# A hybrid decoder layer on one core: weight parts kept in DRAM after their first split, modulation tiles moved, eight differences on GpSimd

## The chip, the core and the metric

One core of a Trainium2 chip runs the whole layer. The metric is device time in microseconds, the median of several runs. Five engines work side by side, each through its own queue in order: TensorE (PE), VectorE (DVE), ScalarE (ACT), GpSimd (POOL) and SyncE (SP), which issues every DMA of this kernel, all into one queue.

## What is computed

One decoder layer over 2048 tokens of width 1024, in float32:

```python
mod = silu(c) @ w_ada + b_ada          # six vectors: shift, scale, gate, twice
h = rms_norm(x, ln1_g) * (1 + sc1) + sh1
p = h @ w_in                           # 3600 columns: qa fa ia ga | qb kb vb gb rb
o = concat(hgrn2(qa, fa, ia, ga), gla(qb, kb, vb, gb, rb))   # two gated linear recurrences, 4 heads each
x = x + gt1 * (o @ w_out)
h = rms_norm(x, ln2_g) * (1 + sc2) + sh2
u = causal_dwconv(h @ w_up)            # 5632 columns, 3 taps
a, v = split(u)
x = x + gt2 * ((silu(a) * v) @ w_down)
return rms_norm(x, lnf_g)
```

## The kernel before, in words

**Split operands.** A float32 matrix product is made of three passes. Each operand is cut into a rounded high part and the remainder (`hi`, `lo`), and `split_passes` multiplies hi by hi, hi by lo and lo by hi. `split_into` (L124 to L131) makes the parts: a ScalarE cast (L128) and a VectorE subtraction (L131). Nearly every weight tile is 128 x 1024 (a `ga` tile 128 x 1056), so one weight means one cast and one subtraction, and then 24 matmuls of 512 columns.

**Blocks.** The tokens are worked in four blocks of 512 (`plan_A(s)`, s = 0 to 3), two per half (`sgi`). A block's mixer is a list of steps, made with `add(names, mm, kind)`: `names` are the weights that the step needs, `mm` issues its matmuls. Mixer order: `f0` to `f3`, `ga`, `kb0 qb0 kb1 qb1`, `ia`, `q0`, `vb`, `q1` to `q3`, `gb`, then `o0` to `o7`. `ga`, `ia`, `vb` and `gb` are token sections: four weights, held through four steps, one per group of 128 tokens. Block 0 differs: its `f` and `kb` weights come as eight start tiles `s0` to `s7` (128 x 768, array `ws`), one per 128 rows of the contraction, whose low parts POOL subtracts. So a block has 36 weights of its own, used again in each of the four blocks.

After the mixers of two blocks comes the up-product of that half (`plan_ffn`): five plain feature pairs (`ua`, `uv`, ten weights) for the first block, seventeen pairs for both blocks by Strassen's scheme (kind `"own"`, weights prepared by `weights_first` and its helpers, L1211 and L1215; matmuls L1222), and the same five plain pairs for the second block. Then the down-product, also by Strassen's scheme (L1553), and the final norm (`finish`, L1668). The ten plain weights are thus used four times.

**What sets the order.** `at(i, fn)` hangs other work on step i: the scan stages of the recurrences, norms, gates. ACT and SP issue in program order; DVE, PE and POOL are ordered by the compiler's scheduler, except in the start and the `"own"` steps, which are written out by hand. Weights run through two cursors over the list `seq` of all names: `w_dma(upto)` (L1776) loads raw tiles into the pool `bigp` (12 buffers), `w_split(upto)` (L1791) splits them into the pool `wsp` (4 pairs hi/lo). The main loop (L1872 on) splits what a step needs, for an `"early"` step two more weights before its matmuls, for a `"late"` one after them, and loads up to three raw tiles beyond that. `mid(k)` (L1836) is the same for start step k: it loads the modulation weights of step k+3 (`ada1_load`), raw tile k+4, and splits s(k+1).

**Modulation.** `ada_tile(j, k)` (L227) adds 128 rows of `w_ada` to two accumulators on VectorE (L229), 4 x 8 tiles of two 128 x 512 instructions. `plan_ada` (L1737) hangs the tiles of j = 2 on every second step of block 0 from `ga1`, those of j = 4, 3, 5 on the 24 steps from the second one of block 1; each tile is loaded one step ahead into the pool `slots` (62 buffers of 128 x 512), which nearly all other tiles share.

**Strassen operands.** `build` (L1153) makes sums and differences of the two blocks' normed activations in the four x1 tiles of each block (in `bigp`, loaded by `resid_load` at step `q3`). T3 and T4 are four VectorE differences each (L1171, L1175), then split.

Of the kernel before, what the change touches and what calls it, by code (L numbers as in the profile page):

```python
# [13 lines left out]
ALU = mybir.AluOpType  # L14
# [15 lines left out]
GW = T + RK  # L30
LEAD = 96
WBUF = 1152

EPS = 1e-6
TINY = 2.0 ** -63
# [27 lines left out]
def kernel(  # L63
# [41 lines left out]
    def slot(dt=F32):  # L105
        return slots.tile([P, T], dt, tag="s", name="s")

    def big():
        return bigp.tile([P, 2 * GW], F32, tag="big", name="big")

    def bank():
        return psp.tile([P, T], F32, tag="ps", name="ps")
# [71 lines left out]
    def load_rest():  # L184
        pool.tensor_copy(ones_r, ones)
        sp.dma_start(g2_sb, g2)
        sp.dma_start(lb_sb, lbp)
        gk_raw = slot()[0 : 3 * RK, 0:256]
        sp.dma_start(gk_raw, wgk)
        act.copy(wgk_sb, gk_raw)  # L190
        lo = slice(2 * RK, 3 * RK)
        vec.tensor_tensor(wgk_sb[lo], gk_raw[lo], wgk_sb[lo].bitcast(F32), op=ALU.subtract)
        sp.dma_start(bgk_sb, bgk)
        sp.dma_start(gna_sb, gna)
        sp.dma_start(gnb_sb, gnb)
# [10 lines left out]
        vec.tensor_scalar(omlb, lb_sb, -1.0, 1.0, op0=ALU.mult, op1=ALU.add)  # L206

    ada_acc = {}

# [121 lines left out]
    side = defaultdict(list)  # L331
    inner = defaultdict(list)

    def add(names, mm, kind="early"):

        steps.append((names, mm, kind))
        return len(steps) - 1

    def at(i, fn):
        side[i].append(fn)  # L340
# [432 lines left out]
    def plan_A(s, hurry):  # L773
# [59 lines left out]
        def section(name, banks, src=h):  # L833

            w4 = []
            wide = name == "ga"
            stride = GW if wide else T
            cuts = [(0, T // 2), (T // 2, GW)] if wide else [(0, T)]

            def token(tt):  # L840
                def mm(w):
                    w4.extend(w)
                    pts = [bank() for _ in cuts]
                    m = 0
                    for kp in range(4):
                        if kp == 2:
                            run_half()
                        for k2 in range(2):
                            for hv, wv in split_passes(src[2 * kp + k2], w4[kp]):
                                for pt, (c0, c1) in zip(pts, cuts):  # L850
                                    pe.matmul(  # L851
                                        pt[:, 0 : c1 - c0],
                                        lhsT=hv[:, tt * P : (tt + 1) * P],
                                        rhs=wv[:, k2 * stride + c0 : k2 * stride + c1],
                                        start=(m == 0),
                                        stop=(m == 23),
                                    )
                                m += 1
                    banks.append(pts if wide else pts[0])

                return mm

            for tt in range(NT):
                names = [f"{name}{i}" for i in range(4)] if tt == 0 else []
                tick[f"{name}{tt}"] = add(names, token(tt), "hold" if tt < NT - 1 else "late")

        section("ga", bga)
        for j in range(2):
# [188 lines left out]
        at(tg + 1, u1.stage_f2)  # L1057
        at(tg + 2, lambda: u1.stage_g(oT))

        at(tick["q3"], lambda: resid_load(s))  # L1060

        def out_evac(j):
            xt = x1_of(s, j)
# [23 lines left out]
            return hT[self.s][k]  # L1087

    cap = [None]
    between = []  # L1090

    def names_before(i):
# [2 lines left out]
    def plan_ffn(sg):  # L1095
# [245 lines left out]
        def strassen(f, prev, nxt, nxt2, prev2):  # L1341
# [70 lines left out]
            def t6():  # L1412
# [8 lines left out]
                if nxt2 is not None:  # L1421
                    load_u(nxt2)
                if nxt is None:
                    w_split(cur[1] + 2)

            def s_cap():
                if nxt is None:
                    cap[0] = names_before(info["i1"] + FILL)
                    for k in range(4):
                        back.append(slot())  # L1430
                        sp.dma_start(back[k], h12_d[sg][k])
                    w_dma(cur[1] + 3)

            def t0_():
                s_cap()
# [178 lines left out]
        def unit(u):  # L1614
# [3 lines left out]
            def mm(w):  # L1618
# [29 lines left out]
                        del op[ci, p, k]  # L1648
                if sg == 0 and u == len(units) - 4:
                    cap[0] = None  # L1650
                    w_dma(cur[1] + 2)
                if sg == 0 and u == len(units) - 2:
                    w_split(cur[1] + 2)

            return mm

# [75 lines left out]
        for n in range(4):  # L1732
            at(i1 + n, lambda n=n: norm2_T(s, (2 * n, 2 * n + 1)))

    ada_seq = [(j, k) for j in (2, 4, 3, 5) for k in range(KD)]

    def plan_ada(i0, i1):  # L1737
        def one(j, k):
            if k == 0:
                ada_start(j)  # L1740
            ada_tile(j, k)

        for n, (j, k) in enumerate(ada_seq):
            i = i0 + 2 * n if j == 2 else i1 + n - KD
            at(i - 1, lambda j=j, k=k: ada_load(j, k))
            at(i, lambda j=j, k=k: one(j, k))
            if k == KD - 1:
                at(i + 2, lambda j=j: ada_norm2(j, range(0, 4)))
                at(i + 3, lambda j=j: (ada_norm2(j, range(4, 8)), ada_acc.pop(j)))

    for sgi in range(2):
        s0, s1 = 2 * sgi, 2 * sgi + 1
        tick0, end0 = plan_A(s0, False)
        if sgi == 0:
            plan_ada(tick0["ga0"] + 1, end0 + 1)
        plan_norm1(s1, tick0["gb0"], tick0["gb3"] + 1)
        tick1, end1 = plan_A(s1, True)
        plan_norm2(s0, tick1["gb3"] + 1)
        info = plan_ffn(sgi)
        if sgi == 0:  # L1760
            s2, i5 = s1 + 1, info["last"]
# [12 lines left out]
    RAW_AHEAD, SPLIT_AHEAD = 4, 2  # L1774

    def w_dma(upto):  # L1776
        while cur[0] < min(upto, len(seq) if cap[0] is None else cap[0]):
            i = cur[0]
            t_ = big()
            if seq[i][0] == "s":  # L1780
                t_ = t_[:, 0 : 6 * P]
                sp.dma_start(t_, ws[int(seq[i][1:])])
            elif seq[i][:2] == "ga":
                sp.dma_start(t_, wg[int(seq[i][2:])])
            else:
                t_ = t_[:, 0:D]
# [1 line left out]
            raws[i] = t_  # L1788
            cur[0] += 1

    def w_split(upto):  # L1791
        while cur[1] < min(upto, len(seq) if cap[0] is None else cap[0]):
            i = cur[1]
            w_dma(i + 1)
            hi, lo = (wsp.tile([P, WBUF], F32R, tag=f"w{c}", name=f"w{c}") for c in ("hi", "lo"))
            hi, lo = hi[:, 0 : 2 * GW], lo[:, 0 : 2 * GW]
            raw = raws.pop(i)
            n = raw.shape[-1]
            split_into(hi[:, 0:n], lo[:, 0:n], raw, lo_engine=pool if seq[i][0] == "s" else None)
            wsplit[i] = (hi, lo)  # L1800
            cur[1] += 1


# [11 lines left out]
    with tc.manual_schedule(engines={ENG.Activation, ENG.DVE, ENG.PE, ENG.Pool, ENG.SP}):  # L1815
# [48 lines left out]
        keep_warm(1)  # L1864
        for k in range(KD):
            steps[k][1]([wsplit.pop(k)])
            ptr += 1
        del xn1[0]

    for i, (names, mm, kind) in enumerate(steps):  # L1870
# [7 lines left out]
        if kind == "unit":  # L1878
# [1 line left out]
                fn()  # L1880
            mm(None)
            continue
        w_split(ptr + len(names))
        w = [wsplit.pop(ptr + n) for n in range(len(names))]
        ptr += len(names)
        if kind == "early":
# [6 lines left out]
        run_half()  # L1893
        if kind == "late":
            w_split(ptr + 2)
    for fn in side.pop(len(steps), ()):
# [88 lines left out]
```

## Time and profile before

| | us |
|---|---|
| median of 3 runs (lowest to highest) | 2381.95 (2381.03 to 2382.35) |
| profiled execution, its own time | 2378.33 |
| its span, first to last instruction | 2376.6 |
| mean granted TensorE clock | 0.988 |

PE is matmuls, PEld weight loads; times in rows are microseconds from the span's start, and "mean ns" is that of one instruction. A wait is named by the waiting engine and line, the tile, and what ended it. Matmuls are pipelined and their ends modelled, so the busy time of PE says little; the distance between matmuls says more. In this execution the start and block 0's mixer lie in 0 to 283 us, block 1's mixer in 283 to 537, the first half's plain up-products in 537 to 604, its Strassen part in 604 to 918, the second plain pass in 918 to 976, the down-product to 1200; blocks 2 and 3 lie in 1200 to 1452 and 1452 to 1697, the second half's plain up-products in 1697 to 1765.

### The profile page before, as it was taken

How to read it: one execution, taken by the hardware profiler on the slowest of the kernel's cores; microseconds unless marked ns; L12 is line 12 of the kernel's file. 1: busy time of each engine (PE TensorE's matmuls, PEld its weight loads, DVE VectorE, ACT ScalarE, POOL GpSimd, SP SyncE). 2: the span in 40 equal slices, each digit the busy share in tenths (PEclk: the TensorE clock that was granted, in tenths of full speed). 3: DMA queues.
4: the chain of work that ended last, by engine and by line, in shares of the span. 5: the costliest groups of instructions: out<-in, count | busy, mean ns of one | idle time of the engine just before them, and what ended most of it. 6: DMA issues, size and time to landing. Idle time of an engine off the chain costs nothing.

```text
span 2376.6 us, 33021 instructions
## 1 busy us (share of the span) xinstructions
PE 2299.3 (97%) x12310; PEld 1904.7 (80%) x12310; DVE 1838.8 (77%) x2787; ACT 1179.6 (50%) x2095; POOL 341.0 (14%) x312
## 2 busy tenths in 40 slices
PE   8999999999999999999989999999989999999996
PEld 6878787887788888888777888888878888888885
DVE  6687778868787888987876776577697878897778
ACT  5644544365555455544545454545555455445353
POOL 3342234110000000000224314320100000000001
PEclk9999999999999999999999999999999999999998
DMA  8233353323222247996534124221322222489751
GB/s 307 106 126 116 119 219 105 119 92 134 76 93 102 93 142 250 344 336 217 181 122 159 36 111 170 72 90 54 131 86 94 102 101 101 175 306 375 247 192 71
DMA packets 148705, 360.84 MB, mean 152 GB/s; under 512 B 17544, under 2 KB 20024, under 8 KB 148544
## 3 DMA queue, kind: packets, MB, share of 16 engines
q1 hardware_dynamic: 148544, 358.73, 42.3%
q8 instruction: 96, 1.57, 0.3%
q14 instruction: 65, 0.53, 0.1%
HBM read 293.65 MB, written 65.01 MB: 151 GB/s over the span
## 4 chain that ended last, share of the span: by engine, by line
PE 74%; DVE 16%; ACT 4%; issue 4%; DMA 2%; POOL 0%; SPq 0%; DVEq 0%; ACTq 0%; POOLq 0%
PE ps L1222 26%; PE ps L1553 14%; PE ps L363 13%; PE ps L851 11%; PE ps L886 3%; DVE wlo L131 3%; DVE s L131 2%; DMA s<-in_w_ada 1%; PE ps L709 1%; PE ps L708 1%; ACT whi L128 1%; DVE s L1668 1%; PE ps L682 1%; PE ps L816 1%; DVE s L1579 1%
## 5 line engine op out<-in xcount | busy, mean ns | idle before, releaser
L1222 PE MATMUL ps<-s,whi 128*128 128x512 f32 x1904 | 586.2, 389 | 3.7 <-DVE big L1322 2.4
L363 PE MATMUL ps<-s,whi 128*128 128x512 f32 x1568 | 492.4, 396 | 11.8 <-ACT whi L128 11.8
L131 DVE TENSOR_TENSOR wlo<-big,whi 128x1024 fp32r<-128x1024 f32 (+3 forms) x290 | 343.6, 1194 | 134.4 <-ACT whi L128 130.6
L1222 PEld LDWEIGHTS ps<-s,whi 128*128 128x128 f32 x1904 | 357.0, 188 | 79.2 <-DVE big L1322 3.2
L1553 PE MATMUL ps<-s,whi 128*128 128x512 f32 (+1 forms) x1272 | 385.4, 385 | 4.7 <-DVE s L131 3.0
L1222 PE MATMUL ps<-s,wlo 128*128 128x512 f32 x952 | 369.9, 389 | 2.4 <-DVE wlo L1215 2.4
L363 PEld LDWEIGHTS ps<-s,whi 128*128 128x128 f32 x1568 | 294.9, 190 | 77.6 <-ACT whi L128 14.4
L128 ACT CAST whi<-big 128x1024 fp32r<-128x1024 f32 (+3 forms) x298 | 275.2, 939 | 145.6 <-PE ps L1553 25.5
L851 PE MATMUL ps<-whi,s 128*128 128x512 f32 (+2 forms) x1280 | 339.9, 354 | 5.5 <-ACT whi L128 5.5
L455 POOL TENSOR_TENSOR s<-s 128x512 f32<-128x512 f32 (+1 forms) x69 | 102.8, 1489 | 1545.5 <-DMA big<-in_wd 588.4
L363 PE MATMUL ps<-s,wlo 128*128 128x512 f32 x784 | 307.8, 394 | 3.1 <-DVE wlo L131 3.1
L1553 PEld LDWEIGHTS ps<-s,whi 128*128 128x128 f32 x1272 | 238.3, 190 | 54.0 <-DVE s L131 4.7
L1553 PE MATMUL ps<-s,wlo 128*128 128x512 f32 (+1 forms) x636 | 244.9, 386 | 5.0 <-DVE wlo L131 4.9
L851 PEld LDWEIGHTS ps<-whi,s 128*128 128x128 f32 x1280 | 218.2, 189 | 37.8 <-ACT whi L128 7.2
L851 PE MATMUL ps<-wlo,s 128*128 128x512 f32 (+2 forms) x640 | 205.0, 351 | 6.5 <-DVE wlo L131 6.5
L1222 PEld LDWEIGHTS ps<-s,wlo 128*128 128x128 f32 x952 | 178.7, 188 | 40.4 <-DVE wlo L1215 3.2
L363 PEld LDWEIGHTS ps<-s,wlo 128*128 128x128 f32 x784 | 148.6, 189 | 36.3 <-DVE wlo L131 4.9
L1215 DVE TENSOR_TENSOR wlo<-big,whi 128x1024 fp32r<-128x1024 f32 (+1 forms) x136 | 145.1, 1083 | 5.9 <-ACT whi L1211 5.6
L1211 ACT CAST whi<-big 128x1024 fp32r<-128x1024 f32 (+1 forms) x136 | 127.5, 939 | 37.4 <-DVE big L1199 33.8
L1553 PEld LDWEIGHTS ps<-s,wlo 128*128 128x128 f32 x636 | 120.6, 190 | 30.5 <-DVE wlo L131 7.4
L1267 DVE SCALAR_TENSOR_TENSOR big<-big,cw_sb 128x1024 f32<-128x1024 f32 x68 | 87.3, 1284 | 68.2 <-ACT big L1259 68.2
L851 PEld LDWEIGHTS ps<-wlo,s 128*128 128x128 f32 x640 | 113.6, 189 | 21.9 <-DVE wlo L131 8.5
(220 smaller groups left out, 3277.5 us busy)
## 6 DMA issues: line engine op xcount, KB each, us to landing
big<-in_wt SPq DMA_DIRECT2D x230, 512.0 KB
s<-td SPq DMA_DIRECT2D x110, 256.0 KB
big<-in_wd SPq DMA_DIRECT2D x72, 384.0 KB
s<-actd SPq DMA_DIRECT2D x98, 256.0 KB
s<-in_w_ada SPq DMA_DIRECT2D x96, 256.0 KB
big<-in_wd SPq DMA_DIRECT2D x72, 320.0 KB
actd<-big SPq DMA_DIRECT2D x34, 512.0 KB
td<-s SPq DMA_DIRECT2D x54, 256.0 KB
```

The source lines that it names most:

```text
L128: act.copy(hi, src)
L131: (lo_engine or vec).tensor_tensor(lo, src, hi.bitcast(F32), op=ALU.subtract)
L363: pe.matmul(pt, lhsT=wv[:, k * P : (k + 1) * P], rhs=hv, start=(n == 0), stop=(n == 3 * KD - 1))
L455: engine.tensor_tensor(acc, acc, sq, op=ALU.add)
L682: pe.matmul(ub[lo:hi, p * P : (p + 1) * P], lhsT=self.kt[:, p * P + lo : p * P + hi], rhs=v[p][:, col : col + P], start=True, stop=True,)
L851: pe.matmul(pt[:, 0 : c1 - c0], lhsT=hv[:, tt * P : (tt + 1) * P], rhs=wv[:, k2 * stride + c0 : k2 * stride + c1], start=(m == 0), stop=(m ...
L886: pe.matmul(pout[j][0], lhsT=wv[:, k * P : (k + 1) * P], rhs=hv, start=(k == 0 and m == 0), stop=(k == KD - 1 and m == 2),)
L1211: act.copy(dst[f][0][:, 0:n], src[f][:, 0:n])
L1215: vec.tensor_tensor(lo[:, 0:n], src[f][:, 0:n], hi[:, 0:n].bitcast(F32), op=ALU.subtract)
L1222: pe.matmul(pt, lhsT=wv[:, c0 : c0 + P], rhs=hv, start=(start and n == 0), stop=(n == 11), skip_group_check=not start)
L1267: vec.scalar_tensor_tensor(t_, src[:, 1 : 1 + D], w1, t_, op0=ALU.mult, op1=ALU.add)
L1553: pe.matmul(pt[:, cols], lhsT=wv[:, ki * P : (ki + 1) * P], rhs=hv[:, cols], start=(start and n == 0), stop=(n == 3 * np_ - 1), skip_group ...
```

## The change

Three edits and what they need. **Weights:** at its first use a weight is split as before; SP then stores both parts in DRAM (`w_flush`), and every later use loads the parts instead of the raw tile, with no cast and no subtraction. The start tiles' parts are stored as the `f0` to `f3`, `kb0`, `kb1` tiles that later blocks use, in pieces of 128 columns. Parts go into the four `wsp` pairs and, where `big_pairs` allows (2 or 4 in blocks 1 to 3 and around the plain up-products), into pairs of big buffers; `live` and `last_use` keep account of which step uses a weight last. **Modulation:** the tiles of j = 4, 3, 5 leave out the steps `qb1` to `q0` of block 1 and go on later instead; accumulators are opened two steps ahead. **Differences:** T3 and T4 of the first half are computed by POOL. Also: `resid_load` moves from `q3` to `gb0`, one buffer less in `slots`, big buffers of 1088 columns.

```diff
-    slots = ctx.enter_context(tc.tile_pool(name="slots", bufs=62))
+    slots = ctx.enter_context(tc.tile_pool(name="slots", bufs=61))
...
-        add(["o0", "o1"], parts((0, 1), (0, 1)))
-        add(["o2", "o3"], parts((2, 3), (0, 1)), "hold")
+        add(["o0", "o1"], parts((0, 1), (0, 1)), last=(3, 4))
+        add(["o2", "o3"], parts((2, 3), (0, 1)), "hold", last=(4, 5))
...
-        at(tick["q3"], lambda: resid_load(s))
+        at(tick["gb0"], lambda: resid_load(s))
+        at(tick["gb0"], lambda: big_pairs.__setitem__(0, 2))
+        if s:
+            at(base, lambda: big_pairs.__setitem__(0, 2 if s % 2 else 4))
+        at(end, lambda: big_pairs.__setitem__(0, 0))
...
+            spare = vec if sg else pool
...
-                    vec.tensor_tensor(src[k], x1_of(s1, k + 4), src[k], op=ALU.subtract)
+                    spare.tensor_tensor(src[k], x1_of(s1, k + 4), src[k], op=ALU.subtract)
...
-                    vec.tensor_tensor(src[k], src[k], s0k[k], op=ALU.subtract)
+                    spare.tensor_tensor(src[k], src[k], s0k[k], op=ALU.subtract)
...
-            plan_ada(tick0["ga0"] + 1, end0 + 1)
+            plan_ada((2,), range(tick0["ga0"] + 1, end0, 2))
...
+            busy = range(tick1["qb1"], tick1["q0"] + 1)
+            plan_ada((4, 3, 5), [i for i in range(end0 + 1, end1) if i not in busy])
...
+    START = [f"f{h}" for h in range(4)] + ["kb0", "kb1"]
+    ws_d = [dram.tile([P, 6, D], F32, name=f"wsd{c}") for c in range(2)]
...
+    def w_flush(n=None):
+        for dst, src in wstores[:n]:
+            sp.dma_start(dst, src.bitcast(F32))
+        del wstores[:n]
...
+    def w_load_one(i, bigs_only=False):
+        kinds = list(live.values())
+        if kinds.count("wsp") < 4 and not bigs_only:
+            live[i] = "wsp"
+            hl = [wsp.tile([P, WBUF], F32R, tag=f"w{c}", name=f"w{c}") for c in ("hi", "lo")]
+        elif kinds.count("big") < big_pairs[0]:
+            live[i] = "big"
+            hl = [big(F32R) for _ in range(2)]
+        else:
+            return False
...
+            sp.dma_start(t_.bitcast(F32), src)
...
+    def w_load(bigs_only=False):
+        while cur[1] < limit() and is_loaded(cur[1]) and w_load_one(cur[1], bigs_only):
+            cur[1] += 1
+            cur[0] = max(cur[0], cur[1])
...
+            if seq[i][0] == "s":
+                k = int(seq[i][1:])
+                for c, t_ in enumerate((hi, lo)):
+                    wstores.append((ws_d[c][:, :, k * P : (k + 1) * P], t_.rearrange("p (j c) -> p j c", c=P)))
+            elif seq[i] in again:
+                for c, t_ in enumerate((hi, lo)):
+                    wstores.append((part_of(seq[i], c), t_))
...
             w_dma(k + 4)
+            w_flush()
             w_split(k + 2)
...
         w_dma(min(ptr + 4, cur[1] + 3))
+        w_flush(None if steps[i + 1 : i + 2] and steps[i + 1][2] == "own" else stored)
         due.extend(halfway.pop(i, ()))
         mm(w)
         run_half()
+        w_used(i)
+        w_load()
```

## Rows read from the trace of the kernel before

**Rows 1.** The page, part 1: busy us, share of the span, instructions per engine.

```profile
PE 2299.3 (97%) x12310; PEld 1904.7 (80%) x12310; DVE 1838.8 (77%) x2787; ACT 1179.6 (50%) x2095; POOL 341.0 (14%) x312
```

**Rows 2.** Chain of waits in order of time, 601 to 914: start us, us, what.

```profile
601.45 311.75 PE ps L1222 x1374
```

**Rows 3.** Waits of PE, 283 to 604: us in total, times, longest us.

```profile
PE ps L363 <- ACT whi L128: 4.2, 1, 4.2
PE ps L851 <- ACT whi L128: 2.5, 1, 2.5
PE ps L851 <- DVE wlo L131: 2.4, 1, 2.4
...
PE ps L767 <- DVE s L756: 1.0, 1, 1.0
...
PE ps L363 <- DVE wlo L131: 0.3, 1, 0.3
```

**Rows 4.** Waits of PE, 1200 to 1765, the same columns.

```profile
PE ps L363 <- ACT whi L128: 4.9, 2, 4.2
PE ps L851 <- DVE wlo L131: 4.1, 3, 1.4
PE ps L851 <- ACT whi L128: 3.0, 4, 1.3
PE ps L767 <- DVE s L756: 2.3, 2, 1.4
PE ps L363 <- DVE wlo L131: 1.8, 1, 1.8
PE ps L1222 <- DVE wlo L1215: 1.2, 1, 1.2
PE ps L1222 <- ACT whi L1211: 1.2, 1, 1.2
```

**Rows 5.** Groups of instructions: count | busy us, mean ns | idle before us, what ended it.

```profile
L131 DVE TENSOR_TENSOR wlo<-big,whi 128x1024 fp32r<-128x1024 f32 x162 | 214.8, 1342 | 65.0 <-ACT whi L128 61.6
...
L128 ACT CAST whi<-big 128x1024 fp32r<-128x1024 f32 x162 | 164.4, 1042 | 31.3 <-PE ps L363 18.0 <-PE ps L851 10.2 <-DMA big<-in_wt 3.0
...
L1171 DVE TENSOR_TENSOR big<-big 128x512 f32<-128x512 f32 x8 | 5.5, 682 | 0.0
```

**Rows 6.** Windows: us; PE, PEld, DVE, ACT, POOL busy; PEclk, DMA share, GB/s.

```profile
283.00:537.00 254.00, 246.94 (x1654) 208.98 (x1653) 191.96 (x328) 118.08 (x241) 70.80 (x64) 0.99 0.40 142
915.00:976.00 61.00, 59.82 (x264) 49.20 (x264) 57.41 (x84) 31.99 (x51) 10.70 (x7) 1.00 0.84 290
361.40:368.20 6.80, 5.39 (x14) 4.27 (x15) 6.80 (x9) 0.29 (x1) 3.38 (x4) 0.50 0.12 39
583.20:590.00 6.80, 5.25 (x12) 4.01 (x13) 6.68 (x13) 5.87 (x9) 0.00 (x0) 0.50 0.18 50
1743.80:1747.20 3.40, 3.11 (x7) 2.35 (x8) 3.28 (x8) 3.40 (x7) 0.00 (x0) 0.50 0.00 0
```

**Rows 7.** Transfers, 8 to 40 us: queue, packets, MB, share of 16 engines.

```profile
q1 hardware_dynamic: 6491, 12.71, 104.0%
```

**Rows 8.** Timeline of ACT at 583 us: start us, us, instruction, idle before.

```profile
583.13 0.63 ACT L1127 ACTIVATE s<-s 128x512 f32<-128x512 f32 x1 [6.78 <-DVE s L1123]
```

**Rows 9.** Timeline at 259 us, DVE and POOL.

```profile
259.69 3.45 DVE L131 TENSOR_TENSOR wlo<-big,whi 128x1024 fp32r<-128x1024 f32 x2
...
259.91 4.37 POOL L455 TENSOR_TENSOR s<-s 128x512 f32<-128x512 f32 x2 [39.00 <-ACT s L454]
```

**Rows 10.** Timeline of DVE at 553 us.

```profile
553.04 2.36 DVE L131 TENSOR_TENSOR wlo<-big,whi 128x1024 fp32r<-128x1024 f32 x2
```

**Rows 11.** Timeline of ACT at 48 us.

```profile
48.34 0.91 ACT L269 ACTIVATE s<-s,c_sb 128x256 f32<-128x256 f32 x2
```

**Rows 12.** Waits of SP's queue, 283 to 537: us in total, times, longest us.

```profile
SPq L224 <- PE ps L658: 11.5, 1, 11.5
```

More of the change, by code (lines that the diff above doesn't have):

```diff
@@ L32 @@
 WBUF = 1152
+BBUF = 1088
 EPS = 1e-6
@@ L106, in slot, with big @@
         return slots.tile([P, T], dt, tag="s", name="s")
-    def big():
-        return bigp.tile([P, 2 * GW], F32, tag="big", name="big")
+    def big(dt=F32):
+        return bigp.tile([P, BBUF], dt, tag="big", name="big")
     def bank():
@@ L332, with add @@
     inner = defaultdict(list)
-    def add(names, mm, kind="early"):
+    last_use = {}
+    def add(names, mm, kind="early", last=0):
         steps.append((names, mm, kind))
+        n0 = sum(len(st[0]) for st in steps[:-1])
+        for n in range(len(names)):
+            last_use[n0 + n] = len(steps) - 1 + (last[n] if isinstance(last, tuple) else last)
         return len(steps) - 1
@@ L864, in section @@
                 names = [f"{name}{i}" for i in range(4)] if tt == 0 else []
-                tick[f"{name}{tt}"] = add(names, token(tt), "hold" if tt < NT - 1 else "late")
+                tick[f"{name}{tt}"] = add(names, token(tt), "hold" if tt < NT - 1 else "late", NT - 1)
         section("ga", bga)
@@ L1089 @@
     cap = [None]
+    big_pairs = [0]
     between = []
@@ L1650, in mm @@
                     cap[0] = None
-                    w_dma(cur[1] + 2)
-                if sg == 0 and u == len(units) - 2:
-                    w_split(cur[1] + 2)
+                    big_pairs[0] = 4
+                    w_load(bigs_only=True)
             return mm
@@ L1733, in plan_norm2, with plan_ada @@
             at(i1 + n, lambda n=n: norm2_T(s, (2 * n, 2 * n + 1)))
[L1735 to L1749, printed above, removed]
+    def plan_ada(js, at_steps):
+        it = iter(at_steps)
+        for j in js:
+            for k in range(KD):
+                i = next(it)
+                if k == 0 and j != 2:
+                    at(i - 2, lambda j=j: ada_start(j))
+                at(i - 1, lambda j=j, k=k: ada_load(j, k))
+                at(i, lambda j=j, k=k: ada_tile(j, k))
+            at(i + 2, lambda j=j: ada_norm2(j, range(0, 4)))
+            at(i + 3, lambda j=j: (ada_norm2(j, range(4, 8)), ada_acc.pop(j)))
     for sgi in range(2):
@@ L1773, with part_of, is_loaded, limit @@
     cur = [0, 0]
-    RAW_AHEAD, SPLIT_AHEAD = 4, 2
+    START = [f"f{h}" for h in range(4)] + ["kb0", "kb1"]
+    ws_d = [dram.tile([P, 6, D], F32, name=f"wsd{c}") for c in range(2)]
+    parts_d = {}
+    first_use = {}
+    for i, n in enumerate(seq):
+        first_use.setdefault(n, i)
+    again = set()
+    for i, n in enumerate(seq):
+        if n in START or first_use[n] != i:
+            again.add(n)
+    def part_of(n, c):
+        if n in START:
+            return ws_d[c][:, START.index(n)]
+        if (n, c) not in parts_d:
+            w = 2 * GW if n[:2] == "ga" else D
+            parts_d[n, c] = dram.tile([P, w], F32, name=f"wp{n}_{c}")
+        return parts_d[n, c]
+    def is_loaded(i):
+        return seq[i][0] != "s" and (seq[i] in START or first_use[seq[i]] != i)
+    live = {}
+    now = [0]
+    wstores = []
+    def w_flush(n=None):
+        for dst, src in wstores[:n]:
+            sp.dma_start(dst, src.bitcast(F32))
+        del wstores[:n]
+    def limit():
+        return len(seq) if cap[0] is None else cap[0]
+    def w_used(step):
+        for i in [i for i in live if last_use[i] <= step]:
+            del live[i]
+    def w_load_one(i, bigs_only=False):
[8 more added lines that the diff above has]
+            return False
+        res = []
+        for c, t_ in enumerate(hl):
+            src = part_of(seq[i], c)
+            t_ = t_[:, 0 : src.shape[-1]]
+            sp.dma_start(t_.bitcast(F32), src)
+            res.append(t_)
+        wsplit[i] = tuple(res)
+        return True
+    def w_load(bigs_only=False):
+        while cur[1] < limit() and is_loaded(cur[1]) and w_load_one(cur[1], bigs_only):
+            cur[1] += 1
+            cur[0] = max(cur[0], cur[1])
     def w_dma(upto):
-        while cur[0] < min(upto, len(seq) if cap[0] is None else cap[0]):
+        while cur[0] < min(upto, limit()):
             i = cur[0]
+            if is_loaded(i):
+                break
             t_ = big()
@@ L1789, in w_dma, with w_split @@
             cur[0] += 1
-    def w_split(upto):
-        while cur[1] < min(upto, len(seq) if cap[0] is None else cap[0]):
+    def w_split(upto, need=False):
+        while cur[1] < min(upto, limit()):
             i = cur[1]
+            if is_loaded(i):
+                if not w_load_one(i):
+                    assert not need, seq[i]
+                    return
+                cur[1] += 1
+                cur[0] = max(cur[0], cur[1])
+                continue
             w_dma(i + 1)
             hi, lo = (wsp.tile([P, WBUF], F32R, tag=f"w{c}", name=f"w{c}") for c in ("hi", "lo"))
-            hi, lo = hi[:, 0 : 2 * GW], lo[:, 0 : 2 * GW]
             raw = raws.pop(i)
             n = raw.shape[-1]
-            split_into(hi[:, 0:n], lo[:, 0:n], raw, lo_engine=pool if seq[i][0] == "s" else None)
+            hi, lo = hi[:, 0:n], lo[:, 0:n]
+            split_into(hi, lo, raw, lo_engine=pool if seq[i][0] == "s" else None)
+            live[i] = "wsp"
             wsplit[i] = (hi, lo)
+            if seq[i][0] == "s":
[5 more added lines that the diff above has]
+                    wstores.append((part_of(seq[i], c), t_))
             cur[1] += 1
@@ L1882 @@
             continue
-        w_split(ptr + len(names))
+        stored = len(wstores)
+        w_split(ptr + len(names), True)
         w = [wsplit.pop(ptr + n) for n in range(len(names))]
```

9 lines of the change are left out of this document (7 added, 2 removed).

## The prediction

> **What bounds the kernel now.** The page's busy line comes first: TensorE 97%, VectorE 77%, ScalarE 50% [rows 1]. The 97% overstates how full TensorE is, because matmuls overlap; the chain of waits gives the pace. In the first half's Strassen blocks 1374 matmuls follow one another in 311.75 us, 0.227 us each [rows 2]: nothing but TensorE is left there, and a change can only save in the other stretches. So the third view is the list of who ended TensorE's idle time, by stretch. In 283 to 604 us (mixer of block 1, then the plain up-products) and in 1200 to 1765 us (mixers of blocks 2 and 3, plain up-products of the second half) most of that time ends at a cast (`whi`, line 128) or a subtraction (`wlo`, line 131) that splits a weight [rows 3, 4]. The work behind these waits is 1.34 us of VectorE and 1.04 us of ScalarE per weight [rows 5]. The last view is the windows with the granted clock: around such waits the clock stands at 0.5, the 1.2 GHz level, for 3.4 or 6.8 us [rows 6].
>
> **The change, part by part.**
>
> *Splits removed.* Blocks 1 to 3 each use 36 mixer weights that block 0 has used before, and the up-products use ten weights four times, so 3 x 36 + 3 x 10 = 138 casts and 138 subtractions go: 138 x 1.34 = 185 us of VectorE and 138 x 1.04 = 144 us of ScalarE [rows 5]. Almost all of it lies beside TensorE's work; what counts is the waits. Of weights that will be loaded as parts, 283 to 537 us has 2.5 + 2.4 + 0.3 = 5.2 us (the 4.2 us on line 363 in the same view is a first use and stays split) [rows 3], and 1200 to 1765 us has 4.9 + 4.1 + 3.0 + 1.8 = 13.8 us [rows 4]. Together **-19.0 us**.
>
> *The clock.* Four stretches at half clock follow those waits: one of 6.8 us and three of 3.4 us (from 361.4, 1204.5, 1286.4 and 1743.8 us; the first and the last are shown) [rows 6]. TensorE is busy for most of them, and each busy microsecond at 1.2 GHz does half a microsecond's work: 17 us / 2, less the idle part, **-8 us**. They go only if nothing else idles TensorE just before.
>
> *Waits on a less loaded VectorE.* In the same stretches line 767 waits 1.0 + 2.3 us for gated outputs, and line 1222 1.2 + 1.2 us for the first Strassen weights of the second half [rows 3, 4]. In front of both, the two engines have weight splits in their queues, four `o` weights or the plain weights. Bounds 0 and -5.7 us; I take half, **-3 us**, because the gate's own chain of sigmoid, product and transpose stays.
>
> *What takes the splits' place.* SyncE now issues two part loads per weight, 1.05 MB against 0.52 MB. With the transfer engines full they move 12.71 MB in 32 us, 397 GB/s [rows 7], so a pair of parts takes 2.6 us, while its 24 matmuls take 24 x 0.227 = 5.4 us [rows 2]. The mixer of block 1 moves 142 GB/s now [rows 6]; 36 x 0.52 MB more in 254 us makes 216. The densest stretch is the plain up-products at 915 to 976 us, 290 GB/s [rows 6]: 10 x 0.52 MB more gives 376, below 397. The Trainium skill ("DMA: Bandwidth & Descriptors", Specifications) puts a core's share of HBM at about 358 GB/s; by that figure this pass would end some 3 us late, an estimate, but the row gives 397 and decides. The loads are asked for up to six or eight weights ahead (four pairs, and two or four in big buffers). A section's four pairs come free one by one during its last token step, as each weight's last matmul is done, so a burst starts about 4 us before the section ends. Queued behind a part load that waits for TensorE are the next modulation tiles, the x1 stores and, in the up-products, the stores of activations; VectorE waits for the first of these. Bounds: 0, and for each of the 12 token sections of blocks 1 to 3 one pair's 2.6 us, 31 us. I take **+1 us**: the nearest rows are today's raw weights, asked for about as far ahead, and no wait of TensorE there ends at a load [rows 3, 4]; besides, the modulation tiles leave out the steps (`qb1` to `q0`) in which SyncE would sit on a slot.
>
> *Stores in the first 60 us.* The eight start weights are stored as parts in rows of 512 bytes, 0.79 MB per weight, in the same queue as the loads, which is full from 8 to 40 us (104% of its 16 engines) [rows 7]. Four of these pairs go ahead of the last modulation load (mid(0) to mid(3)): 4 x 0.79 MB / 397 GB/s = 7.9 us if short rows cost nothing extra. I count that load as landed when the full stretch ends, at 40 us; it is first read at 48.34 us [rows 11], so 8 us are covered. Lower bound 0. Upper bound: each 512-byte packet costs what the mean packet of that stretch costs (32 us x 1.04 x 16 engines / 6491 packets = 82 ns) [rows 7], 1536 packets / 16 x 82 ns = 7.9 us per weight, four of them 31 us, less 8, +23 us. I take **+2 us**, near the lower end, since packets of different size do not cost the same. The other stores, 30 weights of block 0 and ten of the first plain pass at 1.05 MB each, lie beside matmuls; a pair is reused four weights later, 4 x 5.4 us on, against 2.6 us for its store. I take **+1 us**, bounds 0 and +5 (two stores' time).
>
> *Eight differences by Pool* (T3 and T4, first half only). VectorE loses 8 x 0.68 = 5.4 us [rows 5] at a place where it decides: ScalarE sat 6.78 us until VectorE's convolution was done (583.13 us) [rows 8], and only then cast the weights for which TensorE waited 4.2 us [rows 3], with 6.8 us of half clock on top [rows 6]. But Pool and VectorE hinder each other. Two subtractions took 3.45 us beside Pool's additions [rows 9] and 2.36 us without [rows 10]: 1.1 us for one encounter. Eight would cost 8.7 us, net +3.3; with none it is -5.4. The Trainium skill ("SBUF — State Buffer", Who interferes with whom) says that a VectorE instruction with two SBUF inputs and a GpSimd one that reads SBUF exclude each other for a whole instruction; the rows agree in kind. The convolutions read PSUM, so part of the encounters fall away. I take **0**, between the ends.
>
> *Modulation tiles and other moves.* The same 24 x 2 products are spread over steps that had none; the residual loads move one step later, past q3. No wait of TensorE names either: 0, with +/-2.
>
> **Sum.** -19 - 8 - 3 + 1 + 2 + 1 + 0 = -26 us against the profiled execution's 2378.3 us (span 2376.6): 2352.3. The median of the runs lies 3.6 us above that execution, so I forecast **2356 us**. Differences within 0.2%, 4.8 us, I call no change, about what a measurement here can tell.
>
> **Rivals.**
>
> *A. The waits move.* With splits gone, TensorE meets the scan chain, which is just behind: the gate, `sprev`, the transposes. For it: line 767 waits already now [rows 3, 4]. Against: VectorE is freed of 185 us. If half of the 19 + 8 us come back, 2356 + 13.5 = 2369. Chance 0.17.
>
> *B. Pool holds VectorE.* The differences run back to back while VectorE is saturated, each one holding it for its whole length; TensorE's 4.2 us wait grows. By the rows +3.3 us, with a longer half clock of 3.4 us: 2363. By the rule that the Trainium skill states there, taken literally, VectorE loses the time of eight whole Pool instructions (4.37 / 2 = 2.19 us each beside VectorE [rows 9]), 17.5 us, less 5.4: +12, 2368. Chance 0.15.
>
> *C. The start is held by the short-row stores:* halfway to the upper bound, +10 us, 2366. For it: the queue is full [rows 7]. Chance 0.10.
>
> *D. Slower: part loads come late.* SyncE issues in order. A modulation tile waited up to 11.5 us for a slot in block 1 [rows 12]; a part load queued behind it starts late, and TensorE then waits at the head of a token section. One pair (2.6 us) plus the half clock after it (1.7 us of loss) at each of 12 sections is 52 us: 2356 + 52 = 2408. It decides from 26 / 12 = 2.2 us per section on. Against: the six steps left out, and the lead of 4 us. Chance 0.12.
>
> *E. Nothing moves:* the waits were only the last of several, within 5 us of 2382. Chance 0.06.
>
> My forecast itself has 0.40: 2345 to 2363 by its own bounds.
>
> **How the numbers follow.** Faster is the forecast with A, B and C: 0.82, less 0.01 for their upper tails, 0.81. Same is E with that tail, 0.07. Slower is D, 0.12. The range runs down to 2336 (the +4 us of costs not paid, the other 2.7 us of the freed waits, 5.4 us by the differences and with them the rest of the first half's plain wait and its clock, some 7 us) and up to 2384, just beyond E's middle; D's case lies outside.
>
> **What would show it.** Right: lines 128 and 131 at 128x1024 fall from 162 to 36 instructions; TensorE's waits on `whi` and `wlo` of lines 363 and 851 are gone outside block 0 and the first plain pass; the four half-clock stretches are missing; HBM traffic grows by 138 x 0.52 MB read and some 48 MB written, 120 MB; what now lies in 283 to 537 us is some 8 us shorter (5.2 of waits, 2.7 of clock), what lies in 1200 to 1765 us some 18 to 20. Wrong: TensorE waits whose releaser is a load of a part (D); a start weight's step later than 65 us (C); a wait longer than 4.2 us before the first Strassen block (B); line 767 or 709 waiting more than now (A).

## The result and the profile after

The changed kernel takes **2354.66 us** (median of 4 runs, 2350.73 to 2356.85) against 2381.49 us in the same measurement (4 runs): ratio 0.9889, 95% interval 0.9877 to 0.9900, so 1.0 to 1.2% less. The forecast was 2356. Its profiled execution took 2356.09 us, span 2354.0.

The page of the changed kernel, part 1 and the traffic of part 3, against [rows 1]:

```profile
PE 2291.7 (97%) x12310; PEld 1904.2 (81%) x12310; DVE 1672.2 (71%) x2641; ACT 1050.9 (45%) x1957; POOL 333.0 (14%) x320
HBM read 366.20 MB, written 113.38 MB: 204 GB/s over the span
```

The page of before has 293.65 MB read and 65.01 written, so traffic grows by 72.6 + 48.4 = 121 MB. VectorE loses 167 us of work and ScalarE 129 (the prediction had 185 and 144 for the splits); the span loses 22.6. The groups of 128 x 1024 splits, against [rows 5] (lines of the layer's code stand 1 to 14 lower in the file than before: 128 is 129, 851 is 858, 1553 is 1567):

```profile
L132 DVE TENSOR_TENSOR wlo<-big,whi 128x1024 fp32r<-128x1024 f32 x36 | 48.2, 1360 | 10.8 <-ACT whi L129 9.4 <-DMA wpua<-whi 0.7 <-ACT big L538 0.3
L129 ACT CAST whi<-big 128x1024 fp32r<-128x1024 f32 x36 | 36.5, 1042 | 11.8 <-DMA big<-in_wt 5.3 <-PE ps L370 4.6 <-PE ps L858 1.1
```

Both traces hold 12310 matmuls, so they can be cut at the same ones in order of time. The stretches below are those of the front part; lengths in us, by the prediction's own terms.

| stretch (before) | before | after | found | forecast |
|---|---|---|---|---|
| start, 2 to 66 | 63.8 | 64.4 | +0.6 | +2 |
| block 0, 66 to 283 | 217.0 | 221.9 | +4.9 | +1 |
| block 1, 283 to 537 | 254.0 | 247.9 | -6.1 | some -8 |
| plain up-products, 537 to 604 | 67.0 | 71.1 | +4.1 | 0 |
| Strassen, 604 to 918 | 313.9 | 313.9 | 0.0 | 0 |
| plain pass and down-product, 918 to 1200 | 282.4 | 283.1 | +0.7 | 0 |
| blocks 2, 3 and plain, 1200 to 1765 | 564.6 | 539.3 | -25.3 | -18 to -20 |
| the rest | 611.6 | 610.3 | -1.3 | 0 |

The spans of these two executions differ by 22.6 us, their own times by 22.2, where the prediction's sum, which starts from this execution of the kernel before, has 26. The medians differ by 26.8: the traced execution of before lies 3.2 us under its median, that of after 1.4 above, and this difference is in no stretch of the table. No stretch with a large term came out exactly: more was saved behind 1200 us, and 9 us were given back in two places that the prediction had put at 1 and 0.

Waits of PE in the changed kernel, 288 to 604 us (us in total, times, longest), against [rows 3]:

```profile
PE ps L370 <- ACT whi L129: 9.8, 1, 9.8
PE ps L715 <- DVE s L679: 2.5, 1, 2.5
PE ps L619 <- POOL s L601: 0.7, 2, 0.4
...
PE ps L774 <- DVE s L763: 0.2, 1, 0.2
```

The 5.2 us for weights that now come as parts (lines 851 and 363 before, 858 and 370 now) are gone. New is a wait for masked scores (line 679), and the wait of 4.2 us before the first Strassen block is now 9.8. The same view of 1204 to 1744 us, against [rows 4]:

```profile
PE ps L476 <- DVE s L132: 1.1, 2, 0.9
PE ps L1235 <- ACT whi L1224: 1.0, 1, 1.0
PE ps L619 <- POOL s L601: 0.7, 2, 0.4
PE ps L774 <- DVE s L763: 0.2, 1, 0.2
```

All 13.8 us of weight waits are gone here. Windows of the changed kernel, columns as in [rows 6]:

```profile
582.10:595.80 13.70, 6.20 (x14) 4.63 (x15) 13.58 (x25) 5.93 (x9) 1.26 (x1) 0.50 0.32 107
141.80:148.60 6.80, 6.58 (x24) 4.72 (x25) 5.17 (x8) 0.00 (x0) 2.01 (x2) 0.50 1.00 392
288.40:536.30 247.90, 243.96 (x1654) 206.84 (x1653) 148.04 (x295) 85.55 (x208) 59.18 (x62) 1.00 0.62 226
921.30:978.10 56.80, 56.80 (x251) 46.86 (x250) 41.57 (x72) 21.14 (x35) 10.07 (x7) 1.00 0.99 366
```

The four half-clock stretches that the prediction named are gone, but the one before the first Strassen block has doubled to 13.7 us, and block 0 has one of 6.8 us at 141.8, where the kernel before has one of 3.4 us at 129.3. Block 1 moves 226 GB/s (216 forecast). The densest pass runs at 366 GB/s with the transfer engines 99% busy and TensorE without a gap: 56.8 us, shorter than the 58.1 before. The 358 GB/s of the Trainium skill ("DMA: Bandwidth & Descriptors", Specifications), by which the prediction's estimate had it end 3 us late, are exceeded without harm.

### The profile page after: what moved, and what is told of

Same layout as the page of the kernel before. It is cut to its first block, busy times and chain, and to the rows that moved or that the text cites. A ratio compares the mean times of both kernels' runs of the same rounds, so it can differ in the third digit from the quotient of the medians.

```text
span 2354.0 us, 32995 instructions
## 1 busy us (share of the span) xinstructions
PE 2291.7 (97%) x12310; PEld 1904.2 (81%) x12310; DVE 1672.2 (71%) x2641; ACT 1050.9 (45%) x1957; POOL 333.0 (14%) x320
## 5 line engine op out<-in xcount | busy, mean ns | idle before, releaser
L1235 PE MATMUL ps<-s,whi 128*128 128x512 f32 x1904 | 586.2, 389 | 1.0 <-ACT whi L1224 1.0
L1235 PEld LDWEIGHTS ps<-s,whi 128*128 128x128 f32 x1904 | 357.2, 188 | 76.1 <-ACT whi L1224 1.4
L1235 PE MATMUL ps<-s,wlo 128*128 128x512 f32 x952 | 369.8, 389 | 0.0
L370 PE MATMUL ps<-s,whi 128*128 128x512 f32 x1040 | 325.5, 395 | 10.8 <-ACT whi L129 10.8
L1567 PEld LDWEIGHTS ps<-s,whi 128*128 128x128 f32 x1272 | 239.3, 190 | 55.9 <-DVE s L132 4.7
L858 PE MATMUL ps<-whi,s 128*128 128x512 f32 (+1 forms) x992 | 252.6, 345 | 0.0
L370 PEld LDWEIGHTS ps<-s,whi 128*128 128x128 f32 x1040 | 194.4, 189 | 53.3 <-ACT whi L129 12.0
L132 DVE TENSOR_TENSOR wlo<-big,whi 128x768 fp32r<-128x768 f32 (+3 forms) x152 | 161.8, 1070 | 73.7 <-ACT whi L129 71.8
L1235 PEld LDWEIGHTS ps<-s,wlo 128*128 128x128 f32 x952 | 178.7, 188 | 36.9
L370 PE MATMUL ps<-s,wlo 128*128 128x512 f32 x520 | 203.4, 392 | 1.5 <-DVE wlo L132 1.5
L370 PE MATMUL ps<-s,big 128*128 128x512 f32 x792 | 185.6, 391 | 0.0
L129 ACT CAST whi<-big 128x768 fp32r<-128x768 f32 (+3 forms) x160 | 134.5, 848 | 106.5 <-DVE big L1548 26.3
L370 PEld LDWEIGHTS ps<-s,big 128*128 128x128 f32 x792 | 147.8, 188 | 31.7 <-issue 1.3
L858 PE MATMUL ps<-wlo,s 128*128 128x512 f32 (+2 forms) x496 | 150.3, 341 | 3.1 <-DVE wlo L132 3.1
L1567 PEld LDWEIGHTS ps<-s,wlo 128*128 128x128 f32 x636 | 120.9, 190 | 29.9 <-DVE wlo L132 6.7
```

What stands on the lines that cost most here:

```text
L129: act.copy(hi, src)
L132: (lo_engine or vec).tensor_tensor(lo, src, hi.bitcast(F32), op=ALU.subtract)
L370: pe.matmul(pt, lhsT=wv[:, k * P : (k + 1) * P], rhs=hv, start=(n == 0), stop=(n == 3 * KD - 1))
L858: pe.matmul(pt[:, 0 : c1 - c0], lhsT=hv[:, tt * P : (tt + 1) * P], rhs=wv[:, k2 * stride + c0 : k2 * stride + c1], start=(m == 0), stop=(m ...
L1235: pe.matmul(pt, lhsT=wv[:, c0 : c0 + P], rhs=hv, start=(start and n == 0), stop=(n == 11), skip_group_check=not start)
L1567: pe.matmul(pt[:, cols], lhsT=wv[:, ki * P : (ki + 1) * P], rhs=hv[:, cols], start=(start and n == 0), stop=(n == 3 * np_ - 1), skip_group ...
```

## Experiments

Each kernel was timed in alternation with the kernel before (2380 to 2382 us in each group of runs); intervals of 95% are those of the ratio to it. A stretch's length is from one profiled execution; lengths of the start differ by up to 4 us among these kernels (62.9 to 66.7) with nothing in the edits to explain it, so a difference of that size needs a wait beside it. Expectations name some runs by label: e1_vec is the differences back on VectorE, e4_mod_back the changed kernel with the modulation tiles on their old steps, e8_start4 the accumulators opened earlier.

### The differences back on VectorE

```diff
-            spare = vec if sg else pool
+            spare = vec
```

> The changed kernel with T3 and T4 of the first half back on VectorE. Theory (GpSimd's differences hold VectorE's two-SBUF-input work before the first Strassen block): the wait on line 370 at 589.6 us falls from 9.99 to 4 or 5 us, its half clock from 13.7 to 6.8 us, and the time falls by 4 to 7 us, to 2348 to 2351. Rival (the longer wait comes from the weights' side, stores that hold the pairs): the wait stays at about 10 us or grows by VectorE's 5.4 us, time 2354 to 2360.

2348.81 us, ratio 0.9863 (0.9848 to 0.9879), as the theory has it, and 5.8 us below the changed kernel's median, measured in another group of runs; 537 to 604 us takes 66.9 us instead of 71.1, with this wait and a half-clock stretch of 6.8 us:

```profile
PE ps L370 <- ACT whi L129: 5.3, 1, 5.3
```

The mechanism is in VectorE's timeline. In the changed kernel it does 12 two-operand instructions (sums and low parts) while GpSimd does the eight differences:

```profile
570.30 5.18 DVE L1179 TENSOR_TENSOR big<-big 128x512 f32<-128x512 f32 x3
575.41 1.78 DVE L132 TENSOR_TENSOR s<-big,s 128x512 fp32r<-128x512 f32 x1
577.11 1.77 DVE L1179 TENSOR_TENSOR big<-big 128x512 f32<-128x512 f32 x1
578.80 7.52 DVE L132 TENSOR_TENSOR s<-big,s 128x512 fp32r<-128x512 f32 x7
586.24 0.74 DVE L1131 SCALAR_TENSOR_TENSOR s<-ps,cw_sb,s 128x511 f32<-128x511 f32 x1
```

That is 586.24 - 570.30 = 15.9 us. With the differences on VectorE the same point of its queue comes after 19 instructions (the same 12 and seven of the differences), 571.30 to 582.74 us, 11.4 us, 0.60 each:

```profile
571.30 1.89 DVE L1179 TENSOR_TENSOR big<-big 128x512 f32<-128x512 f32 x3
573.11 0.68 DVE L132 TENSOR_TENSOR s<-big,s 128x512 fp32r<-128x512 f32 x1
573.71 0.68 DVE L1179 TENSOR_TENSOR big<-big 128x512 f32<-128x512 f32 x1
...
582.74 0.74 DVE L1131 SCALAR_TENSOR_TENSOR s<-ps,cw_sb,s 128x511 f32<-128x511 f32 x1
```

So 12 instructions that need 12 x 0.60 = 7.2 us took 15.9: VectorE lost 8.7 us to eight GpSimd instructions, 1.1 us each, which is the prediction's price for one encounter, paid eight times. At this point VectorE is 15.9 - 11.4 = 4.5 us later, and the stretch is 4.2 us longer; the rest of the 5.8 us between the medians the traces do not place.

### The differences alone

The kernel before, with T3 and T4 of the first half on GpSimd and nothing else.

> The kernel before with the eight differences on GpSimd and nothing else. Theory (GpSimd holds VectorE): slower by 4 to 7 us, 2385 to 2389, all of it between 580 and 605 us. The prediction's term: 0, 2381.5, with bounds 2376 and 2385. By the rule of whole-instruction exclusion taken literally: +12, 2393.

2384.31 us, ratio 1.0010 (1.0001 to 1.0020): slower by 0.2 to 4.8 us. The stretch 537 to 604 us grows by 3.3 us, and TensorE's wait there from 4.2 to 9.3:

```profile
PE ps L363 <- ACT whi L128: 9.3, 1, 9.3
```

The median lies just under the theory's range, and 3.3 us is the prediction's upper bound: eight encounters at 1.1 us less the 5.4 us that VectorE no longer works. The traces also say where the 1.1 us come from. In the changed kernel's stretch, shown above, VectorE's instructions start 1.70 us apart (575.41, 577.11, 578.80), though each needs only 0.60: about 1.1 us of a GpSimd instruction goes between two of VectorE's. With VectorE idle, GpSimd adds two tiles of the same size in 1.29 us:

```profile
274.54 1.29 POOL L462 TENSOR_TENSOR s<-s 128x512 f32<-128x512 f32 x1 [2.66 <-ACT s L461]
```

So the two take turns, each for nearly a whole instruction. The rule of the Trainium skill ("SBUF — State Buffer", Who interferes with whom) fits this in kind, and nearly in size. The 17.5 us that the prediction drew from it used 2.19 us per GpSimd instruction, a length taken beside VectorE that by this reading contains GpSimd's own waiting; eight times 1.29 are 10.3 us, and the trace has 8.7.

### The modulation tiles, without the parts and with them

First the kernel before with the modulation tiles on their new steps; then the changed kernel with the tiles on their old steps. Both runs move the opening of the accumulators together with the tiles.

```diff
-            plan_ada(tick0["ga0"] + 1, end0 + 1)
+            plan_ada((2,), range(tick0["ga0"] + 1, end0, 2))
...
+            plan_ada((4, 3, 5), [i for i in range(end0 + 1, end1) if i not in busy])
```

> The kernel before with the modulation tiles' new steps alone (accumulators opened two steps ahead). The prediction's term: 0 within 2 us, 2379.5 to 2383.5. Rival (the new waits of the changed kernel at 430 and 490 us come from tiles that now lie beside the output projection's chain): 2 to 4 us slower in 283 to 537 us. Second rival (VectorE freed in the scans' steps): 2 to 5 us faster there.

> The changed kernel with the modulation tiles on their old steps. The prediction's term: 0 within 2 us, 2352.5 to 2356.5. Rival (SyncE sits on a slot for a modulation tile in the steps qb1 to q0 and part loads queue behind it): TensorE waits for part loads in block 1, 5 to 12 us slower, 2360 to 2367.

Moved alone: 2380.52 us, ratio 0.9998 (0.9989 to 1.0006), no difference. Taken back in the changed kernel: 2365.63 us, ratio 0.9933 (0.9920 to 0.9947), 11 us slower than with the move. Block 1 takes 259.6 us instead of 247.9 (248.1 to 253.1 in the four other kernels with the move and the start's stores). The size fits the rival, but its form does not: no wait of TensorE ends at a part load. Waits of PE with the tiles back, 283 to 540 us:

```profile
PE ps L618 <- POOL s L600: 5.5, 1, 5.5
PE ps L714 <- DVE s L678: 4.2, 2, 3.7
```

These lines belong to the scans. Line 618 waits for a GpSimd product that VectorE feeds, and VectorE is late because it waits for modulation loads. Waits of VectorE for these in block 1, first in the kernel before (283 to 537 us), then with the tiles back (283 to 540 us):

```profile
DVE s L229 <- DMA s<-in_b_ada: 0.6, 1, 0.6
```

```profile
DVE s L230 <- DMA s<-in_b_ada: 17.3, 2, 9.5
DVE s L230 <- DMA s<-in_w_ada: 6.2, 3, 2.3
```

The longest of these waits lies just ahead of that scan. SyncE issues its load, the opening of an accumulator, behind ten loads of parts that begin at 329.1 us:

```profile
338.88 1.48 SPq L216 DMA_DIRECT2D s<-in_b_ada  x2
```

```profile
346.18 1.42 DVE L230 SCALAR_TENSOR_TENSOR s<-s,c_sb 128x512 f32<-128x512 f32 x2 [9.50 <-DMA s<-in_b_ada]
```

The GpSimd product in the kernel before, with the tiles back, and in the changed kernel:

```profile
360.73 0.94 POOL L594 TENSOR_TENSOR s<-s,dl 128x256 f32<-128x256 f32 x1
369.66 0.68 POOL L600 TENSOR_TENSOR s<-s,dl 128x256 f32<-128x256 f32 x1
365.00 0.68 POOL L601 TENSOR_TENSOR s<-s,dl 128x256 f32<-128x256 f32 x1
```

Counted from the first matmul of block 1 (283.07, 287.38 and 288.42 us) it ends at 78.6, 83.0 and 77.3 us, and with the tiles back TensorE is ready for it at 77.5. So about 1 us of the 5.5 was there in the kernel before, hidden behind the waits for weights; that much is rival A. Over 4 us are new: part loads have delayed a modulation load, and VectorE the scan. With the move, VectorE goes on 2.6 us earlier at this place and has four modulation products fewer in front of the scan, about 3 us. No run separates the other steps from the earlier opening of the accumulators, and the second wait, on line 714, is not followed further.

### The parts alone

The changed kernel with both other edits taken back (tiles on their old steps, `spare = vec`).

> The changed kernel with the modulation tiles on their old steps and the differences on VectorE: the stored parts alone. Theory (effects add: the changed kernel 2354.7, 11 us for the tiles from e4_mod_back, less 5.8 for the differences from e1_vec): 2358 to 2362, so the parts alone save 21 us and the waits of block 1 only move to the scan chain. The prediction's sum without its zero terms: -26, 2355.5, with block 1 shorter than before by some 8 us.

2362.45 us, ratio 0.9928 (0.9916 to 0.9941): half a microsecond above the range for adding effects, 7 above the prediction's. Block 1 takes 259.3 us, **longer** than the 254.0 before, although its weight waits are gone. Waits of PE, 285 to 550 us:

```profile
PE ps L618 <- POOL s L600: 5.0, 1, 5.0
PE ps L714 <- DVE s L678: 4.1, 2, 3.7
```

VectorE stands 9.0 us for the same accumulator's load here.

From 1200 us on this kernel is as fast as the changed one (539.4 against 539.3 us for blocks 2, 3 and the plain pass), where no modulation tiles lie.

### Start parts not stored

`START` is empty: nothing is stored in the start, and `f0` to `f3`, `kb0`, `kb1` are split once more in block 1.

> The changed kernel without the stores of the start tiles' parts; f0 to f3, kb0 and kb1 are split in block 1, stored there, and loaded as parts in blocks 2 and 3 only. Theory (the short-row stores cost the start nothing that shows): the first 66 us keep their length within 1 us, block 1 is 0 to 5 us longer for six splits more, total 2353 to 2360. Rival C (the start is held by those stores): the first 66 us are 3 to 10 us shorter, total 2345 to 2352.

2367.88 us, ratio 0.9946 (0.9932 to 0.9960), 13 us slower than the changed kernel, more than either expected. The start is no shorter (66.7 us), so rival C is out. The first half of block 1 (to 412 us) grows from 123.8 to 140.8 us. Waits of PE, 283 to 430 us:

```profile
PE ps L619 <- POOL s L601: 7.6, 1, 7.6
PE ps L988 <- DVE s L983: 4.5, 1, 4.5
```

With six splits in front of the scans the scans are late again, by 12 us of waits, and no wait of TensorE in block 1 is for a weight. The stores of the start are worth their traffic for that, not for any wait on a weight.

### No lead for the parts

```diff
-        at(tick["gb0"], lambda: big_pairs.__setitem__(0, 2))
+        at(tick["gb0"], lambda: big_pairs.__setitem__(0, 0))
```

and likewise wherever `big_pairs` is set: parts go into the four pairs only.

> The changed kernel with parts loaded into the four pairs alone, none into big buffers. Theory (the four pairs come free about 4 us before a section ends, a pair's load takes 2.6 us): 0 to 5 us slower, 2354 to 2360. Rival D (part loads come late once the lead is gone): TensorE waits for loads of parts at the heads of the token sections, up to 2.6 us and half a clock stretch of 1.7 us at each of 12 of them, 10 to 50 us slower, 2365 to 2405.

2375.03 us, ratio 0.9972 (0.9959 to 0.9985), 20 us slower than the changed kernel. Now TensorE's releasers are loads. Waits of PE, 283 to 2340 us:

```profile
PE ps L893 <- DMA whi<-wpo: 2.0, 3, 0.8
PE ps L370 <- DMA wlo<-wpua: 1.8, 4, 0.5
PE ps L370 <- DMA whi<-wpua: 1.3, 2, 0.9
...
PE ps L370 <- DMA wlo<-wsd: 1.0, 3, 0.5
...
PE ps L858 <- DMA whi<-wpga: 0.6, 1, 0.6
...
PE ps L858 <- DMA wlo<-wpvb: 0.3, 1, 0.3
```

The pair-by-pair handover costs up to 0.9 us at a time, not the 2.6 + 1.7 us at each of 12 sections of rival D. These waits sum to 7 us; the rest of the 20 is spread over stretches (second plain pass 62.2 us against 56.8, most of block 2 192.8 against 188.9), and this run does not divide it further. The total lies in rival D's range, by a smaller price per wait than its own. In the changed kernel no wait of TensorE behind the start ends at a load: the big buffers keep these waits away.

### Stores without use

The kernel before with all stores of parts added, which nothing reads.

> The kernel before with the stores of the parts added and nothing else: the stored parts are never read. The prediction's terms: +2 us in the start, +1 in block 0 and the first plain pass, 2384.5 against 2381.5. Theory after the changed kernel's trace: the start within 1 us, block 0 longer by 1.5 to 5 us because a split must wait for the store of the pair that it overwrites, 2383 to 2386. Rival (block 0's 4.9 us are a clock stretch that comes with a small shift of TensorE against VectorE, and stores cost nothing): 2380.5 to 2382.5.

2386.51 us, ratio 1.0024 (1.0015 to 1.0033), slower by 3.6 to 7.9 us: just above the theory's range, and for another reason than the theory's. The start keeps its length (64.0); block 0 takes 222.7 us instead of 217.0. Issues on SyncE, and VectorE, at the place of the first loss:

```profile
79.14 0.70 SPq L215 DMA_DIRECT2D s<-in_b_ada  x2
79.94 0.36 SPq L1785 DMA_DIRECT2D wpga<-whi  x1
...
84.15 1.16 SPq L1785 DMA_DIRECT2D wpga<-wlo  x1
85.36 3.52 SPq L224 DMA_DIRECT2D s<-in_w_ada  x4
```

```profile
90.97 0.75 DVE L229 SCALAR_TENSOR_TENSOR s<-s,c_sb 128x512 f32<-128x512 f32 x1 [6.68 <-DMA s<-in_w_ada]
```

SyncE sits on opening an accumulator (line 215), issues the stores of the `ga` parts, and only then the modulation tiles, at 85.4 us (77.8 before). VectorE stands 6.68 us for the tile with the low parts of the next weights queued behind it, and TensorE waits 3.4 us for one of those. The changed kernel opens that accumulator in the start; there VectorE stands only 0.6 us at this place. The two runs above with stores and the old opening (tiles back, parts alone) take 222.3 and 223.8 us for block 0 as well. So this is the wait of the modulation tiles' runs once more: there the loads stood behind part loads, here behind stores.

### Accumulators opened earlier

On top of the kernel with the differences on VectorE:

```diff
-                    at(i - 2, lambda j=j: ada_start(j))
+                    at(i - 4, lambda j=j: ada_start(j))
```

> The kernel of e1_vec with the accumulators of j = 4, 3, 5 opened four steps ahead of their first tile instead of two. Theory (the two clears of an accumulator, 0.98 us on GpSimd, stand in front of the clear that the masked scores of line 679 wait for, and TensorE's 2.7 us wait on line 715 with the half clock after it comes from that): that wait falls under 2 us, 1 to 5 us faster than e1_vec, 2344 to 2348. Rival (line 679 waits for the scores themselves): no change, 2347.5 to 2350.

**2344.77 us**, ratio 0.9845 (0.9832 to 0.9859). The wait for masked scores falls from 2.5 to 1.6 us, as the clear (line 674) no longer stands behind the accumulator's (line 216). GpSimd in the changed kernel:

```profile
426.44 0.98 POOL L216 MEMSET s<- 128x512 f32 x2
427.37 0.52 POOL L674 MEMSET s<- 128x512 f32 x1
```

The interval overlaps that of the differences on VectorE alone. Of the 4.0 us between the two, the trace ties 0.9 us to the edit; the half-clock stretch behind that wait was 10.2 us there, 3.4 here, and none in the changed kernel with the same wait, so it isn't shown that it went with the edit. Both edits together beat the changed kernel: the intervals do not overlap.

### Activation behind the casts

On top of the last one, the activation and product of a plain up-product are issued one step later, behind the next two casts.

> The kernel of e8_start4 with the sigmoid-linear unit and the product of a plain up-product, in the passes over a half's first block, issued one step later, behind the casts of the next two weights. Theory (the weight wait before the first Strassen block is made by ScalarE's order: the casts stand behind an activation that waits for VectorE's 11 us of operand sums): the wait of about 5 us on line 370 and its 6.8 us at half clock go, 5 to 8 us faster than e8_start4, 2337 to 2340. Rival (VectorE is full there, so the low parts come late anyway and the wait moves to wlo or to the first Strassen weights): 0 to 2 us, 2343 to 2345.

2343.78 us, ratio 0.9848 (0.9834 to 0.9861): no difference, the rival. The stretch gains 1.4 us (65.6 against 67.0), because the wait only changes its name:

```profile
PE ps L370 <- DVE wlo L132: 4.3, 1, 4.3
```

The cast is no longer late, but the low part is: VectorE itself is full there, busy for 14.40 of the 14.40 us up to this wait.

## Why the prediction was right, and where it was not

**Total:** -26.8 us between medians against -26, but 22.2 between the traced executions. Much of the agreement is luck: errors of both signs, and 4.6 us that no stretch shows.

**Splits removed, the clock, and the waits on a less loaded VectorE (-19, -8, -3).** Right from 1200 us on, and a little small. The 13.8 us of weight waits went with three half-clock stretches (10.2 / 2 = 5.1 us); of lines 767 and 1222 the waits fell from 4.7 to 1.2 us, 3.5 where I had taken half. That is 22.4 of the 25.3 us found; another 0.9 us on line 991 went as well, and 2 to 3 us have no name. The -3 term was thus too small in this place. In block 1 the same terms came true only by grace of another part: -6.1 us with the moved tiles (-0.9 to -5.8 in the four other kernels that have them and the start's stores), +5.4 without.

**Modulation tiles (0).** This is the step that failed: "No wait of TensorE names either: 0". True of the kernel before (moved alone: no difference) and wrong of the changed one, where the move, with the earlier opening of the accumulators, is worth 11 us. The 0 was read from a trace without part loads, in which VectorE stands 0.6 us for modulation loads in block 1; with part loads in the same queue and the tiles on their old steps it stands 23.5. The term on the part loads had named this wait ("VectorE waits for the first of these") but took its +1 from TensorE's waits, and gave the moved tiles no price. Rival A, in which the scan chain was just behind all along, holds for about 1 us of the 5.5 that TensorE then waits for GpSimd.

**Eight differences (0).** Mis-sized: alone +3.4 us, at the upper bound of +3.3, and +4.2 in its stretch of the changed kernel. The reason for halving it, that convolutions read PSUM, did not apply: the differences ran beside 12 instructions with two SBUF operands, and each difference cost one encounter. Rival B's place, wait and longer clock stretch all came, as a cost inside the sum.

**Stores (+2, +1).** The start: near 0, and nothing to gain by dropping them. Transfers of the changed kernel from 8 to 40 us, columns as in [rows 7]:

```profile
q1 hardware_dynamic: 10081, 12.43, 106.8%
```

Nearly the same 12.4 MB in 55% more packets: the short ones did not cost what the mean packet costs, as the lower bound had it.

Block 0: +4.9 us in this execution, with 6.8 us at half clock near 141 us. Of the six kernels with stores and moved tiles two have 6.8 us there (220.7 and 221.9 us), four have 3.4 or none (216.1 to 218.8, 217.5 on average); the three without stores took 216.3 on average. So about +1, and up to the +5 of the bound when the clock falls. With the old accumulator opening the stores cost 4.9 us on the whole.

**Part loads (+1).** 0 on TensorE in this kernel, because of the big buffers; 20 us without them. What the loads did to VectorE's modulation loads is told above. The reason given, four pairs free about 4 us early, was not enough by itself.

## What to carry to other kernels

Before an edit is costed at nothing because no wait names it, ask what the other edits of the same change add to the queues that it uses: here new loads made old ones late, and moving the work that waits for those was worth 11 us beside the stored parts and nothing alone. Price such parts alone and together. Work moved from VectorE to GpSimd saved nothing here, where VectorE's own instructions beside it have two SBUF operands: count one encounter, 1.1 us in this form, per moved instruction. And in a queue that issues in order, look at what stands behind a new store or load, not only at its bandwidth.

## Unexpected of the hardware

A half-clock stretch is not a fixed price of a wait. After the same wait of 2.5 us on line 715 the records show 10.2 us at half clock with the differences back on VectorE, 3.4 without the lead for the parts, and none in the changed kernel. The first of these, columns as in [rows 6]:

```profile
425.90:436.10 10.20, 9.20 (x74) 8.16 (x75) 6.08 (x17) 2.69 (x18) 1.10 (x3) 0.50 0.42 151
```

So executions can differ by 2 to 5 us in a stretch that waits the same, and a stretch should be compared in several kernels before its few microseconds are explained. Whether two executions of one kernel differ in this way isn't shown: each kernel here has one trace.
